# The up-projection of a gated MLP as seven half-size block products, with its weights split once and kept in DRAM

## The chip, the cores and the metric

The kernel runs on one core of one Trainium2 chip. The metric is the device time of one execution in microseconds (us); a profile of one execution shows what each engine did: TensorE (PE, its weight loads PEld), VectorE (DVE), ScalarE (ACT), GpSimd (POOL) and the DMA queue of SyncE (SP).

## The reference, cut to what matters

One layer: token mixing (projections, sparse attention, a pooling mixer, an output projection), a LayerNorm, then the part that the change rewrites:

```
def conv_ffn(x, conv_w, conv_b, w_up, w_down):
    h = x @ w_up                                     # (2048,1024) @ (1024,5632)
    h = causal depthwise conv, width 3, over time (h) + conv_b
    gate, val = jnp.split(h, 2, axis=-1)
    return (jax.nn.silu(gate) * val) @ w_down        # (2048,2816) @ (2816,1024)
x = layer_norm(ALPHA * x + ffn, ln2_g, ln2_b)
```

All is float32. The kernel takes each float32 operand as two fp32r parts, high and low, and makes every product of three matmuls (high by high, high by low, low by high): `mm3`, line 311.

## The kernel before, in words

The stages follow one another: projections, attention (`attention`, line 1193), the output projection with the first LayerNorm (`mix_out`, line 1249), the MLP (`ffn`, line 1398). Each stage is a Python generator that emits instructions for all engines in one order, and every engine runs its own in that order. `big` is a pool of 42 SBUF buffers of 4 KB a partition from which nearly all tiles come (`T`, line 260); a DMA load on SP can start when its buffer has been left by the last reader. PSUM is eight banks: four single ones (`PS1`, line 276) and two pairs (`PS2`, line 279). A result that goes to DRAM is put on a list by `store` and issued on SP two calls of `turn` later (lines 317 and 332).

**Attention.** For each block of 128 queries and each half of the heads (a unit) `values` (line 1094) walks over the key blocks, one step each, 272 steps in all: PE transposes the weights, ACT and DVE split them, PE multiplies by the values; the scores of the next unit are made between. POOL splits queries and outputs, and widens the reciprocal sums that PE transposes in `tail` (line 1119). The selection of the last key blocks, on DVE and ACT, is still under way when attention starts.

**The end of the output projection.** For the last 512 rows `mix_out` goes row block by row block; between them `ffn_ahead` (line 1321) loads rows of the normed x, transposes them on PE and splits them.

**The MLP.** The 2048 tokens are done in two halves of 1024. For each of the NF = 22 blocks f of 128 hidden channels, PE projects gate and value (`project`, 2 parts x 2 groups of 512 tokens x 8 slices of 128 input channels x 3 = 96 matmuls), ACT and DVE make the convolution out of PSUM (`conv`), ACT the SiLU, POOL the product with the value and its low part (`hidden`). Then `down` multiplies the block before by its rows of w_down (8 row blocks x 2 column groups x 3 = 48 matmuls), and DVE adds each 128x512 result from PSUM to a sum in SBUF. The up and down weights are loaded from the inputs for each half and split, mostly by POOL. At the change of halves the next rows are transposed beside the last `down`, and the norms of the first half (`norm_stages`, line 1358) run beside the first blocks of the second.

## Time and profile before

| | |
|---|---|
| median of 3 runs | 3420.83 us (3418.41 to 3428.26) |
| profiled execution, its span | 3423.1 us |
| its engines, busy | PE 3310.3, PEld 2802.5, DVE 2211.0, ACT 1345.0, POOL 1107.0 us |
| DMA | 399.51 MB, 117 GB/s over the span |

The profiled execution is known by its span, 3423.1 us from the first to the last instruction; it lies among the three timed runs, 2.3 us over their median. Busy time of PE is modelled for pipelined matmuls, so idle time before an instruction, with what ended it, says more than a busy share.

### The profile page before, as it was taken

How to read it: one execution, taken by the hardware profiler on the slowest of the kernel's cores; microseconds unless marked ns; L12 is line 12 of the kernel's file. 1: busy time of each engine (PE TensorE's matmuls, PEld its weight loads, DVE VectorE, ACT ScalarE, POOL GpSimd, SP SyncE). 2: the span in 40 equal slices, each digit the busy share in tenths (PEclk: the TensorE clock that was granted, in tenths of full speed). 3: DMA queues.
4: the chain of work that ended last, by engine and by line, in shares of the span. 5: the costliest groups of instructions: out<-in, count | busy, mean ns of one | idle time of the engine just before them, and what ended most of it. 6: DMA issues, size and time to landing. Idle time of an engine off the chain costs nothing.

```text
span 3423.1 us, 45344 instructions
## 1 busy us (share of the span) xinstructions
PE 3310.3 (97%) x16710; PEld 2802.5 (82%) x16710; DVE 2211.0 (65%) x4477; ACT 1345.0 (39%) x2520; POOL 1107.0 (32%) x1050
## 2 busy tenths in 40 slices
PE   8997899999999899999999999999999999999997
PEld 8886788888898788888788788888888778888886
DVE  5589878987888877777766544344444745445356
ACT  3466747746776666666410211111111411111113
POOL 3147410010012431111311334453443444354452
PEclk9998899999999999999999999999999999999999
DMA  8457755752765111000533521111112321111111
GB/s 317 139 204 269 254 199 198 267 194 88 277 220 166 62 42 31 30 28 7 201 126 142 188 78 40 53 43 50 56 44 86 129 87 44 50 50 43 56 44 68
DMA packets 237052, 399.51 MB, mean 117 GB/s; under 512 B 14938, under 2 KB 151070, under 8 KB 236830
## 3 DMA queue, kind: packets, MB, share of 16 engines
q1 hardware_dynamic: 227038, 378.79, 32.5%
q10 hardware_dynamic: 9792, 17.83, 1.4%
q8 instruction: 131, 2.15, 0.3%
q14 instruction: 91, 0.75, 0.1%
HBM read 289.44 MB, written 107.12 MB: 116 GB/s over the span
## 4 chain that ended last, share of the span: by engine, by line
PE 69%; DVE 6%; issue 2%; ACT 1%; POOL 1%; DMA 0%; POOLq 0%; SPq 0%; DVEq 0%; ACTq 0%
PE p L134 69%; DVE b L134 4%; DVE m L134 1%; ACT b L134 1%; POOL b L134 0%; DMA q<-m 0%; DMA b<-in_w_ffn_down_dram 0%; POOL nr L134 0%; DVE nt L134 0%; ACT m L134 0%; DVE t L134 0%; DVE nd L134 0%; DVE rinv L134 0%; DVE ab L134 0%; DVE bn L134 0%
## 5 line engine op out<-in xcount | busy, mean ns | idle before, releaser
L134 PE MATMUL p<-b,b 128*128 128x512 f32 (+2 forms) x14448 | 3077.8, 371 | 48.1 <-ACT b L134 21.6
L134 PEld LDWEIGHTS p<-b,b 128*128 128x128 f32 x14448 | 2512.8, 190 | 497.8 <-ACT b L134 24.5
L134 POOL TENSOR_TENSOR b<-b,b 128x1024 fp32r<-128x1024 f32 (+4 forms) x429 | 732.2, 1715 | 730.1 <-DVE b L134 610.9
L134 DVE TENSOR_TENSOR b<-b,p 128x512 f32<-128x512 f32 x608 | 380.9, 685 | 283.5 <-PE p L134 283.4
L134 ACT ACTIVATE b<-p 128x512 fp32r<-128x512 f32 (+9 forms) x658 | 395.3, 622 | 374.1 <-PE p L134 345.2
L134 DVE SCALAR_TENSOR_TENSOR b<-p,cw,b 128x1022 f32<-128x1022 f32 (+4 forms) x188 | 227.9, 1212 | 433.1 <-ACT b L134 432.1
L134 POOL TENSOR_SCALAR b<-b 128x1024 fp32r<-128x1024 f32 (+3 forms) x346 | 260.4, 761 | 646.3 <-ACT b L134 323.1
L134 ACT ACTIVATE b<-p,cw 128x1024 f32<-128x1024 f32 (+1 forms) x94 | 108.3, 1152 | 842.8 <-PE p L134 730.1
L134 ACT ACTIVATE m<-b,F 128x448 bf16<-128x448 f32 (+3 forms) x448 | 365.9, 819 | 81.8 <-DVE F L134 72.0
L134 DVE TENSOR_SCALAR_CACHE_REDUCE m<-b,F 128x512 bf16<-128x512 f32 (+6 forms) x476 | 371.1, 809 | 16.1 <-DMA q<-m 11.3
L134 ACT ACTIVATE b<-b 128x1024 fp32r<-128x1024 f32 (+3 forms) x130 | 130.8, 1011 | 342.2 <-POOL b L134 156.5
L134 DVE TENSOR_TENSOR b<-p,b 128x512 fp32r<-128x512 f32 (+1 forms) x306 | 222.4, 733 | 65.5 <-ACT b L134 62.7
L134 PE MATMUL p<-ident,b 128*128 128x128 f32 x1456 | 216.5, 277 | 21.1 <-ACT b L134 13.6
L134 PEld LDWEIGHTS p<-ident,b 128*128 128x128 f32 x1456 | 176.3, 142 | 55.2 <-ACT b L134 16.1
L134 DVE CUSTOM_DVE_ANT_0 b<-p,b 128x1024 f32<-128x1024 f32 (+7 forms) x192 | 174.3, 909 | 67.8 <-PE p L134 64.7
L134 ACT ACTIVATE b<-b,mx 128x1024 f32<-128x1024 f32 (+7 forms) x192 | 171.4, 895 | 42.6 <-DVE mx L134 37.3
L134 DVE SCALAR_TENSOR_TENSOR b<-b,ws,b 128x768 f32<-128x768 f32 (+5 forms) x154 | 157.2, 1049 | 41.8 <-ACT b L134 39.5
L134 PE MATMUL p<-kst,b 128*128 128x384 f32 (+3 forms) x656 | 150.5, 360 | 4.7 <-DVE b L134 3.6
L134 PEld LDWEIGHTS p<-kst,b 128*128 128x128 f32 x656 | 110.7, 189 | 21.2 <-ACT b L134 7.5
L134 POOL COPY b<-halo 128x16 f32<-128x16 f32 x16 | 2.8, 197 | 307.6 <-PE p L134 307.5
L134 ACT ACTIVATE m<-p 128x512 f32<-128x512 f32 x120 | 69.8, 593 | 76.5 <-PE p L134 61.6
L134 DVE TENSOR_TENSOR b<-b,b 128x1024 fp32r<-128x1024 f32 (+9 forms) x65 | 71.6, 1108 | 30.7 <-ACT b L134 22.6
(109 smaller groups left out, 1210.3 us busy)
## 6 DMA issues: line engine op xcount, KB each, us to landing
b<-wp SPq DMA_DIRECT2D x192, 512.0 KB, 6.0
b<-in_w_ffn_up_dram SPq DMA_DIRECT2D x88, 512.0 KB, 4.5
wp<-b SPq DMA_DIRECT2D x64, 512.0 KB, 5.5
b<-in_w_ffn_down_dram SPq DMA_DIRECT2D x44, 512.0 KB, 3.8
b<-in_w_in_dram SPq DMA_DIRECT2D x32, 512.0 KB, 6.5
xT<-b SPq DMA_DIRECT2D x32, 512.0 KB, 5.7
b<-xT SPq DMA_DIRECT2D x32, 512.0 KB, 6.1
b<-gm SPq DMA_DIRECT2D x32, 512.0 KB, 6.8
```

The lines of the kernel that those rows point to most:

```text
L134: return f(*args, **kw)
```

## The change

**Seven products.** The up-projection of two blocks of 128 hidden channels for 1024 tokens is a 2x2 block product: two halves of the 1024 input channels, two channel blocks, two groups of 512 tokens. Instead of eight block products, Strassen's seven are made: each is 4 slices of 128 input channels x 3 = 12 matmuls on sums or differences of blocks. A unit u is such a pair of channel blocks; a half of the tokens has 22 units (gates and values in turn), 154 products. Four PSUM banks hold the seven: products 5, 4 and 7 accumulate in the banks of 3, 2 and 1 (`BANK`, `OPENS`). `evacuate` puts the outputs together in SBUF on DVE and ACT; the convolution then reads SBUF.

**Sums of x.** For each j of four, `x_turn` transposes two slices of 128 channels for 1024 tokens (16 transposes), and `x_mix` makes the seven operands, sums first, then high and low parts. For the first half this lies in `mix_last`, which replaces the last part of `mix_out`; for the second in the last quarter of `down_half(0)`. The LayerNorm of the last four row blocks moves into the first unit.

**Sums of weights.** `up_weights` makes 154 tiles (22 units x 7, 512 KB each with high and low part) and stores them to DRAM: the first 98 during attention, all on POOL, from three buffers that take the place of constants no longer needed (`early_pool`, `late_pool`); the other 56 during the first up half, 0.6 a product, high parts on ACT. Each product's tile is fetched five products ahead (`up_fetch`), in both halves.

**The hidden channels** go to DRAM (`d_h`, 44 stores of 512 KB). **Down-projection:** `down_half` runs after each up half; for each of 2 x 2 groups of 512 tokens and 512 columns it accumulates over all 22 blocks in PSUM, in four banks, so that the sums in SBUF fall away. Each chunk of h and of w_down (256 KB each) is loaded and split (ACT the high part, DVE and POOL half of the low part each), two chunks ahead. In the very last group the last six blocks are done row block by row block.

The diff, cut to its core; the removed `ffn` is printed with the kernel above:

```diff
+TAIL = ("D--", "A--", "D--", "A--")
+ORDER = (3, 2, 1, 6, 5, 4, 7)
+BANK = {3: 0, 5: 0, 2: 1, 4: 1, 1: 2, 7: 2, 6: 3}
+OPENS = (3, 2, 1, 6)
+X_PLAIN = {2: 0, 5: 3}
+X_SUMS = {3: (1, 3, OP.subtract), 1: (0, 3, OP.add), 6: (1, 0, OP.add), 4: (2, 0, OP.subtract), 7: (2, 3, OP.add)}
+W_PLAIN = {3: 0, 4: 3}
+W_SUMS = {2: (2, 3, OP.add), 1: (0, 3, OP.add), 6: (2, 0, OP.subtract), 5: (0, 1, OP.add), 7: (1, 3, OP.subtract)}
+UP_AHEAD = 5
+W_BEFORE, W_FROM, W_RATE = 14, 4, 0.6
+LASTK = 6
...
     def attention(self):
+        self.early_pool.release()
+        self.late_pool = self.tc.alloc_tile_pool(name="latep", bufs=3)
+        self.w_inside, self.wcredit = W_BEFORE, 0.0
+        self.wgen = self.up_weights()
+        rate = W_BEFORE * len(ORDER) / (self.ends[-1] - W_FROM)
...
+                if tpos > W_FROM:
+                    self.up_more(rate)
...
+    def mix_last(self, mixed, ys, gb):
...
+        self.x_load(0, 0)
+        plan = {(0, 2): [lambda: self.x_turn(0)],
+                (0, 3): self.x_mix(0, 0, 2), (0, 4): self.x_mix(0, 2, 4),
+                (0, 5): self.x_mix(0, 4, 6), (0, 6): self.x_mix(0, 6, 7),
+                (1, 0): [lambda: self.x_load(0, 1)],
+                (1, 2): [lambda: self.x_turn(1)] + self.x_mix(1, 0, 1),
+                (1, 3): self.x_mix(1, 1, 4) + [lambda: self.x_load(0, 2)],
+                (1, 4): self.x_mix(1, 4, 7),
+                (1, 5): [lambda: self.x_turn(2)] + self.x_mix(2, 0, 2) + [lambda: self.x_load(0, 3)],
+                (1, 6): self.x_mix(2, 2, 7) + [lambda: self.up_fetch(0)],
+                (1, 7): [lambda: self.x_turn(3)] + [lambda i=i: self.up_fetch(i) for i in range(1, UP_AHEAD)]}
...
+        for c in range(2):
+            cs = slice(c * 512, (c + 1) * 512)
+            acc = [self.PS1() for _ in range(RB)]
+            for dc in range(DC):
...
+                for f in plan.get((c, dc), ()):
+                    f()
...
+            for rb in range(RB):
+                nc.vector.scalar_tensor_tensor(ys[rb][:, cs], ys[rb][:, cs], ALPHA, acc[rb], op0=OP.mult, op1=OP.add)
+        for f in self.x_mix(3, 0, 7):
+            f()
...
+    def combine(self, t, a, b=None, op=None, add=None, low=None, high=None):
+
+        nc = self.nc
+        if op is not None:
+            s = self.M(list(t.shape[:1]) + list(t.shape[2:]))
+            add.tensor_tensor(s, a, b, op=op)
+            a = s
+        if high is None:
+            nc.scalar.activation(t[:, 0], a, AF.Copy)
+        else:
+            high.tensor_scalar(t[:, 0], a, 1.0, 1.0, op0=OP.mult, op1=OP.mult)
...
+        for r in raw:
+            ps = self.PS2([P, 2, G])
+            for i in range(2):
+                for rb in range(RB):
+                    nc.tensor.transpose(ps[:, i, rb * P:(rb + 1) * P], r[:, i * RB + rb], self.ident)
+            b += [ps[:, 0], ps[:, 1]]
+        for i in (0, 3):
+            s = self.M([P, G])
+            nc.scalar.activation(s, b[i], AF.Copy)
+            b[i] = s
+        self.xsrc[j] = b
...
+            else:
+                t = self.T([P, 2, G], F32R)
+            b = self.xsrc[j]
+            low = nc.gpsimd if m in (2, 5) else nc.vector
+            if m in X_PLAIN:
+                self.combine(t, b[X_PLAIN[m]], low=low)
+            else:
+                i, k, op = X_SUMS[m]
+                self.combine(t, b[i], b[k], op, nc.gpsimd if m == 1 else nc.vector, low)
+            self.xc[m, j] = t
+
+        return [lambda m=m: one(m) for m in ORDER[lo:hi]]
...
+    def up_weights(self):
...
+        nxt = load(0)
+        for n in range(NF):
+            r = nxt
+            a = (r[0][:, :, :P], r[1][:, :, :P], r[0][:, :, P:], r[1][:, :, P:])
+            for s, m in enumerate(ORDER):
+                if s == 4 and n + 1 < NF:
+                    nxt = load(n + 1)
+                inside = n >= self.w_inside
+                t = (self.T if inside else self.L)([P, 2, 4, P], F32R)
+                high = None if inside else nc.gpsimd
+                if m in W_PLAIN:
+                    self.combine(t, a[W_PLAIN[m]], low=nc.gpsimd, high=high)
+                else:
+                    u, v, op = W_SUMS[m]
+                    self.combine(t, a[u], a[v], op, nc.gpsimd, nc.gpsimd, high)
+                self.store(self.d_w[n * len(ORDER) + s], t.bitcast(F32))
+                yield
+
...
+    def up_fetch(self, i):
+        t = self.uw[i] = self.T([P, 2, 4, P], F32R)
+        self.nc.sync.dma_start(t.bitcast(F32), self.d_w[i % len(self.d_w)])
...
+        def product(i, ps, m, js):
...
+            for j in js:
+                x = self.xc[m, j]
+                self.mm3(ps, w[:, 0, j], w[:, 1, j], x[:, 0], x[:, 1], j == 0 and m in OPENS, j == 3, m not in OPENS)
...
+        def evacuate(m, ps, st):
+            if m == 3:
+                st["s3"] = self.M([P, G])
+                nc.scalar.activation(st["s3"], ps, AF.Copy)
+            elif m == 2:
+                st["d"] = self.M([P, G])
+                nc.vector.tensor_tensor(st["d"], st["s3"], ps, op=OP.subtract)
+            elif m == 1:
+                st["e"] = self.M([P, G])
+                nc.vector.tensor_tensor(st["e"], st["d"], ps, op=OP.add)
+            elif m == 6:
+                st["h2"] = self.T([P, 2 * G])
+                nc.vector.tensor_tensor(st["h2"][:, G:], st["e"], ps, op=OP.add)
+            elif m == 5:
+                st["h1"] = self.T([P, 2 * G])
+                nc.scalar.activation(st["h1"][:, G:], ps, AF.Copy)
+                nc.vector.tensor_tensor(st["d"], st["d"], ps, op=OP.subtract)
+            elif m == 4:
+                nc.scalar.activation(st["h2"][:, :G], ps, AF.Copy)
+                nc.vector.tensor_tensor(st["d"], st["d"], ps, op=OP.add)
+            else:
+                nc.vector.tensor_tensor(st["h1"][:, :G], st["d"], ps, op=OP.add)
+
...
+            def first(i):
+                h, ch = st[f"h{i}"], part * NF + 2 * p + i - 1
+                v = a[i] = self.T([P, 2 * G])
+                nc.scalar.activation(v, h, AF.Identity, bias=cw[:, 3, ch:ch + 1], scale=cw[:, 2, ch:ch + 1])
+                nc.vector.scalar_tensor_tensor(v[:, 1:], h[:, :2 * G - 1], cw[:, 1, ch:ch + 1], v[:, 1:],
+                                               op0=OP.mult, op1=OP.add)
...
+            for s, m in enumerate(ORDER):
+                i = n * len(ORDER) + s
+                if i + UP_AHEAD < (hf + 1) * NF * len(ORDER):
+                    self.up_fetch(i + UP_AHEAD)
+                self.up_more(W_RATE)
+                if s in pending:
+                    pending[s]()
+                if u == 0 and s >= 3 and self.unnormed:
+                    self.unnormed.pop(0)()
+                if u == 0 and s < 4:
+                    product(i, banks[BANK[m]], m, range(3))
+                    if s == 3:
+                        for k in range(4):
+                            product(i - 3 + k, banks[BANK[ORDER[k]]], ORDER[k], [3])
+                            evacuate(ORDER[k], banks[BANK[ORDER[k]]], st)
+                else:
+                    product(i, banks[BANK[m]], m, range(4))
+                    evacuate(m, banks[BANK[m]], st)
+                if u == NF - 1 and s >= 4:
+                    self.down_ahead(hf, s - 4)
+                yield 2.7
+            pending = conv(st, n % 2, u // 2)
+        self.pending = pending
...
+    def down_load(self, hf, i):
+        q, c, k = i // (2 * NF), i // NF % 2, i % NF
+        t = self.draw[i] = self.T([P, 2, G])
+        self.nc.sync.dma_start(t[:, 0], self.d_h[hf][k][:, q * G:(q + 1) * G])
+        self.nc.sync.dma_start(t[:, 1], self.a["w_ffn_down"][0, k * P:(k + 1) * P, c * G:(c + 1) * G])
+
+    def down_split(self, i):
+        nc = self.nc
+        t = self.draw.pop(i)
+        hi, lo = self.T([P, 2, G], F32R), self.T([P, 2, G], F32R)
+        nc.scalar.activation(hi, t, AF.Copy)
+        nc.vector.tensor_tensor(lo[:, 0], t[:, 0], hi[:, 0].bitcast(F32), op=OP.subtract)
+        nc.gpsimd.tensor_tensor(lo[:, 1], t[:, 1], hi[:, 1].bitcast(F32), op=OP.subtract)
+        self.dparts[i] = (hi, lo)
...
+                    part = self.dparts.pop(i)
+                    if final and k >= NF - LASTK:
+                        held.append((k, part))
+                    else:
+                        for rb in range(RB):
+                            down(acc, k, rb, part)
+                    if hf == 0 and q == 1 and c == 1:
+                        for f in self.ahead_up.get(k, ()):
+                            f()
+                    norm_tick()
+                    if not held:
+                        yield 2.7
+                for rb in range(RB):
...
+                    nc.vector.scalar_tensor_tensor(ys[rb][:, cs], ys[rb][:, cs], ALPHA, acc[rb], op0=OP.mult, op1=OP.add)
+                    if c == 1:
+                        norm((hf * 2 + q) * RB + rb, ys[rb], TAIL[rb] if final else "A--")
+                    if held:
+                        yield 2.7
+        if hf == 0:
+            for f in self.x_mix(3, 0, 7):
+                f()
+        while norming:
+            norm_tick()
+            yield 1.0
...
+    def ffn(self):
+        yield from self.up_half(0)
+        n = NF * len(ORDER)
+        self.ahead_up = {1: [lambda: self.x_load(1, 0)], 3: [lambda: self.x_turn(0)], 4: self.x_mix(0, 0, 3),
+                         5: self.x_mix(0, 3, 5) + [lambda: self.x_load(1, 1)], 6: self.x_mix(0, 5, 7),
+                         8: [lambda: self.x_turn(1)], 9: self.x_mix(1, 0, 3),
+                         10: self.x_mix(1, 3, 5) + [lambda: self.x_load(1, 2)], 11: self.x_mix(1, 5, 7),
+                         13: [lambda: self.x_turn(2)], 14: self.x_mix(2, 0, 3),
+                         15: self.x_mix(2, 3, 5) + [lambda: self.x_load(1, 3)],
+                         16: self.x_mix(2, 5, 7) + [lambda: self.up_fetch(n)],
+                         19: [lambda: self.x_turn(3)],
+                         21: [lambda i=i: self.up_fetch(n + i) for i in range(1, UP_AHEAD)]}
+        yield from self.down_half(0)
+        yield from self.up_half(1)
+        yield from self.down_half(1)
...
-    def ffn(self):
```

## Rows read from the trace of the kernel before

**Rows 1.** The page: busy time, share of the span and instructions of each engine; then the chain of work that ended last, by engine.

```profile
PE 3310.3 (97%) x16710; PEld 2802.5 (82%) x16710; DVE 2211.0 (65%) x4477; ACT 1345.0 (39%) x2520; POOL 1107.0 (32%) x1050
...
PE 69%; DVE 6%; issue 2%; ACT 1%; POOL 1%; DMA 0%; POOLq 0%; SPq 0%; DVEq 0%; ACTq 0%
```

**Rows 2.** Busy time in stretches: attention, the start of the MLP, its first half, the change of halves, the second half, and what follows the last matmul. Columns: us, then busy us (instructions) of PE, PEld, DVE, ACT, POOL, the granted clock, DMA share, GB/s.

```profile
1143.00:1660.00 517.00, 507.32 (x2912) 431.83 (x2911) 382.41 (x774) 332.97 (x636) 118.56 (x112) 0.99 0.12 36
...
1944.00:2000.00 56.00, 52.42 (x235) 42.03 (x234) 25.65 (x32) 14.66 (x24) 18.96 (x15) 0.97 0.39 135
2000.00:2650.00 650.00, 650.00 (x2871) 537.97 (x2870) 295.24 (x401) 97.05 (x124) 302.57 (x162) 1.00 0.18 53
2650.00:2730.00 80.00, 77.15 (x360) 63.28 (x359) 67.41 (x100) 35.14 (x50) 30.20 (x20) 0.98 0.33 110
2730.00:3358.00 628.00, 624.06 (x2748) 513.85 (x2746) 284.47 (x443) 87.22 (x78) 293.07 (x156) 1.00 0.19 57
...
3406.20:3423.10 16.90, 0.00 (x0) 0.00 (x0) 12.17 (x28) 5.65 (x10) 4.58 (x3) 0.60 0.34 135
```

**Rows 3.** Timeline of ACT in the first half of the MLP: the first step of the convolution, which starts when a part's projection is done. Columns: start, us, engine, line, operation, output and input.

```profile
2157.92 1.21 ACT L134 ACTIVATE b<-p,cw 128x1024 f32<-128x1024 f32 x1 [5.93 <-issue]
2179.66 1.21 ACT L134 ACTIVATE b<-p,cw 128x1024 f32<-128x1024 f32 x1 [13.79 <-PE p L134]
...
2190.59 1.21 ACT L134 ACTIVATE b<-p,cw 128x1024 f32<-128x1024 f32 x1 [5.93 <-issue]
```

**Rows 4.** All waits of PE from 1900 us to the end: total us, times, longest.

```profile
PE p L134 <- DVE b L134: 5.1, 4, 2.7
PE p L134 <- POOL b L134: 2.8, 3, 1.3
PE p L134 <- ACT b L134: 2.4, 2, 1.2
```

**Rows 5.** Groups of DVE instructions, forms apart: busy us, mean ns of one, idle before.

```profile
L134 DVE TENSOR_TENSOR b<-b,p 128x512 f32<-128x512 f32 x608 | 380.9, 685 | 283.5 <-PE p L134 283.4
L134 DVE TENSOR_TENSOR b<-p,b 128x512 fp32r<-128x512 f32 x280 | 190.8, 688 | 54.5 <-ACT b L134 51.9
L134 DVE SCALAR_TENSOR_TENSOR b<-p,cw,b 128x1023 f32<-128x1023 f32 x82 | 105.2, 1283 | 403.8 <-ACT b L134 403.8
L134 DVE SCALAR_TENSOR_TENSOR b<-b,nr,b 128x1024 f32<-128x1024 f32 x14 | 22.1, 1588 | 0.1
```

**Rows 6.** The same for ACT.

```profile
L134 ACT ACTIVATE b<-p,cw 128x1024 f32<-128x1024 f32 x82 | 99.0, 1207 | 787.4 <-PE p L134 674.7 <-issue 112.7
...
L134 ACT ACTIVATE b<-b 128x1024 f32<-128x1024 f32 x41 | 43.3, 1056 | 63.2 <-DVE b L134 58.4 <-DVE nt L134 4.8
L134 ACT ACTIVATE b<-p 128x512 f32<-128x512 f32 x64 | 37.6, 593 | 23.0 <-PE p L134 15.3 <-issue 6.5 <-ACT b L134 0.2
...
L134 ACT ACTIVATE m<-b,nm 128x1024 bf16<-128x1024 f32 x14 | 16.1, 1147 | 14.9 <-DVE nm L134 14.8
L134 ACT ACTIVATE m<-b 128x1024 bf16<-128x1024 f32 x14 | 14.7, 1048 | 8.4 <-DVE b L134 8.2
```

**Rows 7.** The same for POOL.

```profile
L134 POOL TENSOR_TENSOR b<-b,b 128x512 fp32r<-128x512 f32 x30 | 38.8, 1293 | 2.4
L134 POOL TENSOR_SCALAR b<-b 128x512 fp32r<-128x512 f32 x30 | 23.0, 766 | 321.6 <-ACT b L134 321.6
...
L134 POOL TENSOR_TENSOR nr<-nv,mhalf 128x1 f32<-128x1 f32 x16 | 14.7, 919 | 82.8 <-DVE nm L134 59.8 <-DVE nv L134 23.0
L134 POOL COPY m<-rinv 128x256 f32<-128x256 f32 x32 | 12.6, 413 | 42.6 <-DVE rinv L134 42.6
```

**Rows 8.** Timeline in attention: POOL's widening of the sums for a `tail`, and PE's transposes of it.

```profile
1351.09 0.75 POOL L134 COPY m<-rinv 128x256 f32<-128x256 f32 x2
...
1352.88 0.60 PE L134 MATMUL p<-ident,m 128*128 128x128 f32 x4
```

**Rows 9.** Timeline at the start of attention: DVE instructions with two inputs in SBUF beside POOL's, and PE after them (in brackets, its idle time and what ended it).

```profile
1159.98 2.34 POOL L134 TENSOR_TENSOR b<-b,b 128x1024 fp32r<-128x1024 f32 x1
1160.15 2.19 DVE L134 TENSOR_TENSOR t<-F,st 128x2 f32<-128x2 f32 x1
...
1163.14 1.94 PE L134 MATMUL p<-b,b 128*128 128x512 f32 x6 [3.08 <-DVE mx L134]
...
1181.38 1.27 POOL L134 TENSOR_TENSOR b<-b,b 128x512 fp32r<-128x512 f32 x1
1181.38 1.28 DVE L134 SCALAR_TENSOR_TENSOR nd<-b,fx,cg 128x1 f32<-128x1 f16 x1
...
1183.32 2.02 PE L134 MATMUL p<-b,b 128*128 128x512 f32 x5 [1.14 <-DVE nd L134]
```

**Rows 10.** One tile in attention, the sum of two partial sums (both in SBUF) on DVE: duration in ns, least, median and most.

```profile
L134 DVE TENSOR_TENSOR rinv<-ssum x16: 156/158/1486, 1284.2 to 1643.2; 128x4 f32<-128x4 f32 x16
```

**Rows 11.** Three stretches of 10 us in which the DMA engines are busy throughout; columns as in Rows 2. In the first, rows of 1 KB are loaded and rows of 4 KB stored, in the second mostly rows of 4 KB are stored, in the third loaded.

```profile
210.00:220.00 10.00, 9.43 (x40) 6.90 (x39) 8.84 (x32) 7.71 (x25) 9.76 (x21) 1.00 1.02 324
320.00:330.00 10.00, 10.00 (x45) 8.26 (x44) 9.82 (x6) 1.92 (x6) 10.00 (x19) 1.00 1.03 415
...
1680.00:1690.00 10.00, 10.00 (x46) 8.29 (x45) 9.28 (x10) 4.29 (x6) 5.93 (x4) 1.00 1.03 413
```

**Rows 12.** DMA issues of the page: output and input, count, size, median us from issue to landing.

```profile
b<-wp SPq DMA_DIRECT2D x192, 512.0 KB, 6.0
b<-in_w_ffn_up_dram SPq DMA_DIRECT2D x88, 512.0 KB, 4.5
```

**Rows 13.** Waits of SP's own DMA queue from 2000 to 3350 us: line, what it waited for, us in total, times, longest.

```profile
SPq L193 <- PE p L134: 1151.6, 77, 22.5
```

More of the change, by code (lines that the diff above doesn't have):

```diff
@@ L271, in C, with E @@
         return self.const.tile(shape, dt, tag=n, name=n)
+    def E(self, shape, dt=F32, name="e"):
+        n = self._name(name)
+        return self.early_pool.tile(shape, dt, tag=n, name=n)
     def sml(self, shape, dt=F32, tag="t", bufs=None):
@@ L309, in split_new, with mm3 @@
         return hi, lo
-    def mm3(self, ps, ah, al, bh, bl, first, last):
+    def mm3(self, ps, ah, al, bh, bl, first, last, more=False):
+        kw = {"skip_group_check": True} if more else {}
         mm = self.nc.tensor.matmul
-        mm(ps, ah, bh, start=first, stop=False)
-        mm(ps, ah, bl, start=False, stop=False)
-        mm(ps, al, bh, start=False, stop=last)
+        mm(ps, ah, bh, start=first, stop=False, **kw)
+        mm(ps, ah, bl, start=False, stop=False, **kw)
+        mm(ps, al, bh, start=False, stop=last, **kw)
     def store(self, dst, src):
@@ L370, in tables @@
         nc.vector.tensor_copy(posf, self.posi)
[L371 removed]
+        inv = self.E([P, ROT], name="inv")
         for i, f in enumerate(FREQS):
@@ L427, in setup @@
         self.d_at = [self.DT([P, 4, G], name="at") for _ in range(NG)]
-        self.d_x1 = [self.DT([P, D], name="x1") for _ in range(NB)]
+        self.d_x1 = [self.DT([NB // 2, P, D], name="x1") for _ in range(2)]
+        self.d_h = [[self.DT([P, 2 * G], name="h") for _ in range(NF)] for _ in range(2)]
         self.I = {}
@@ L1298, in mix_out @@
                 ys.append(y)
-            if g + 1 < NG:
-                nxt = load_at(g + 1)
-            else:
-                pre = Share(self.ffn_ahead(), 7, 5)
+            if g + 1 == NG:
+                yield from self.mix_last(mixed, ys, gb)
+                return
+            nxt = load_at(g + 1)
             for rb in range(RB):
@@ L1347, in ffn_ahead @@
         nc.vector.tensor_copy(self.cw, ps[:, :, :2 * NF])
-        self.xrows = self.x1_rows(0, 1, range(EARLY))
-    def x1_rows(self, hf, q, rbs=range(RB)):
+    def combine(self, t, a, b=None, op=None, add=None, low=None, high=None):
[8 more added lines that the diff above has]
+            high.tensor_scalar(t[:, 0], a, 1.0, 1.0, op0=OP.mult, op1=OP.mult)
+        low.tensor_tensor(t[:, 1], a, t[:, 0].bitcast(F32), op=OP.subtract)
@@ L1351, in x1_rows, with L, x_load @@
+    def L(self, shape, dt):
+        return self.late_pool.tile(shape, dt, tag="l4", name=self._name("l"))
+    def x_load(self, hf, j):
         t = []
-        for rb in rbs:
-            r = self.T([P, D])
-            self.nc.sync.dma_start(r, self.d_x1[hf * 8 + q * RB + rb])
+        for k in (j, j + 4):
+            r = self.T([P, NB // 2, P])
+            self.nc.sync.dma_start(r, self.d_x1[hf][:, :, k * P:(k + 1) * P].rearrange("b p c -> p b c"))
             t.append(r)
-        return t
+        self.xraw[j] = t
@@ new lines, in x_turn @@
+    def x_turn(self, j):
+        nc = self.nc
+        raw = self.xraw.pop(j)
+        b = []
+        for r in raw:
[9 more added lines that the diff above has]
+        self.xsrc[j] = b
@@ new lines, in x_mix, with one @@
+    def x_mix(self, j, lo, hi):
+        def one(m):
+            nc = self.nc
+            if m == 7 and j < 3:
+                t = self.L([P, 2, G], F32R)
+            else:
[9 more added lines that the diff above has]
+        return [lambda m=m: one(m) for m in ORDER[lo:hi]]
@@ new lines, in up_weights, with load @@
+    def up_weights(self):
+        nc = self.nc
+        up = self.a["w_ffn_up"][0].rearrange("(k p) c -> p k c", p=P)
+        self.d_w = [self.DT([P, 2, 4, P], name="uw") for _ in range(NF * len(ORDER))]
+        def load(n):
+            c0 = n % 2 * DFF + n // 2 * 2 * P
+            t = [self.T([P, 4, 2 * P]) for _ in range(2)]
+            for k in range(2):
+                nc.sync.dma_start(t[k], up[:, 4 * k:4 * k + 4, c0:c0 + 2 * P])
+            return t
+        nxt = load(0)
[15 more added lines that the diff above has]
+                yield
@@ new lines, in up_more, with down_ahead @@
+    def up_more(self, rate):
+        self.wcredit += rate
+        while self.wcredit >= 1:
+            self.wcredit -= 1
+            next(self.wgen, None)
+    def down_ahead(self, hf, step):
+        if step == 0:
+            self.draw, self.dparts = {}, {}
+        self.down_load(hf, step)
+        if step:
+            self.down_split(step - 1)
+    def down_load(self, hf, i):
[3 more added lines that the diff above has]
+        self.nc.sync.dma_start(t[:, 1], self.a["w_ffn_down"][0, k * P:(k + 1) * P, c * G:(c + 1) * G])
@@ L1613, in run @@
         self.settle()
+        self.late_pool.release()
 @with_exitstack
```

314 lines of the change are left out of this document (110 added, 204 removed).

## The prediction

> **What bounds the kernel now.** I read the page first: PE is busy for 3310 of 3423 us, and the chain that ended last runs through PE for 69% [rows 1]. A share of the whole can hide stages with other limits, so the stretches come next. In attention PE idles 9.7 of 517 us; in the MLP it never waits from 2000 to 2650 us, 2.9 us around the change of halves, 3.9 us in the second half and 3.6 us at the start; then come 16.9 us without matmuls [rows 2]. DVE is busy for less than half of the MLP, DMA for a fifth. So the MLP is PE's alone, and a change is worth what it takes from PE less what it makes PE wait for.
>
> The price of a matmul is not the mean of its row, since pipelined matmuls overlap. The convolution starts at 2157.92 and again at 2190.59 us, one block f later [rows 3]: 32.67 us for 96 + 48 = 144 matmuls of 512 columns, 0.2269 us each. The step for one part alone (48 matmuls, 2179.66 to 2190.59) gives 0.2277, so the up and the down matmuls cost the same.
>
> **The change part by part.**
>
> *Seven for eight.* Before, the up-projection takes 2 x 22 x 96 = 4224 matmuls; after, 2 x 22 x 7 x 12 = 3696. The 2112 of the down-projection stay, the transposes too (64 a half). 528 x 0.2269 = 119.8 us less on PE. The operands keep type and size, so I take the same price.
>
> *Putting the seven together.* A unit lasts 84 x 0.2269 = 19.1 us. DVE has six additions with one operand in PSUM (0.685), four convolution steps from SBUF (taken at the 1.283 of the PSUM form) and one product a unit (taken alike): 4.1 + 5.1 + 1.3 = 10.5 us [rows 5]. ACT has three copies (0.593), two convolution starts (1.207) and one SiLU (1.056): 5.3 us [rows 6]. Units alternate between bank sets, and a bank is used twice inside a unit only three or four products (8 us) apart. Cost on PE: none, with 8.6 us of DVE to spare in each unit; without that cover a late evacuation would stop PE at products 5, 4 or 7.
>
> *Weight sums in attention.* A tile takes POOL 0.766 for the high part, 1.293 for the low part and in five of seven cases 1.293 for the sum: 2.98 us, and 98 tiles 292 us [rows 7]. With the 118.6 us that POOL has there already it is busy for 411 of 517 us [rows 2], so it keeps up. What is queued behind it waits: the copies for `tail` end 1.0 us before PE transposes them [rows 8]. There are 32 copies [rows 7], two a `tail`, so 16 tails. If POOL is inside a weight tile with chance 0.56 and a uniform rest of it delays the copies, PE waits 0.37 us in the mean, 6 us together; bounds 0 and 16 x 2 = 32.
>
> The second price is DVE's. At 1160 us a DVE addition of 128x2, with two inputs in SBUF, lasts 2.19 us beside a POOL instruction of 2.34, and PE then idles 3.08; at 1181 one of 128x1 lasts 1.28 beside one of 1.27, and PE idles 1.14 [rows 9]. POOL will be busier in just that stretch, the end of the selection: I add 5 us (bounds 0 and 15, five such pairs). Later such additions come once a unit, at most 1.49 us for 0.158 [rows 10]; DVE has a quarter of its time free there [rows 2]: 2 us (0 to 8). The Trainium skill (SBUF — State Buffer, Who interferes with whom) gives a rule that speaks against this change: a DVE instruction with two SBUF inputs and a GpSimd instruction that reads SBUF exclude one another for the whole instruction. By that rule the convolution, which moves from PSUM to SBUF, and the low parts become exposed to POOL too, and the additions with an operand in PSUM don't. Attention: +13 us (0 to 55).
>
> *Start of the MLP.* In `mix_last`, the operands of one j take DVE nine instructions of 0.69, ACT nine of 0.6 and POOL three of 1.29. The third j has 5.4 us of PE's work as cover and needs about 8, so `x_turn(3)` waits some 3 us for its banks; then the additions of the last four banks and the fourth j stand on DVE, partly covered by the 36 matmuls (8.2 us) that need only three j. I take 7 us of idle time in place of 3.6: +3.4 (bounds 0 and +10).
>
> *Supply of weights.* Bytes for a product in the first 93: a fetch of 0.524 MB, 0.6 of a store, 0.09 of raw weights, 0.075 of hidden channels: 1.004 MB in 2.723 us, 369 GB/s. Busy DMA engines move 413 to 415 GB/s in rows of 4 KB, 324 with rows of 1 KB among them [rows 11]; nine tenths here are of 4 KB, so I take it as just enough. A fetch issued five products ahead has 13.6 us, against 6.0 to land [rows 12]; but loads on SP wait for buffers that PE leaves [rows 13], and the 42 are nearly all in use, so the lead is shorter. The stores wait on POOL on the same queue, with the fetches behind them. Bounds: 0, and at 324 GB/s 3.098 - 2.723 = 0.375 us for each of 93 products, 35 us. I take +3, near the rows of 4 KB. The Trainium skill (HBM Reference, Specifications (TRN2)) gives an effective 358 GB/s per core; this trace shows more, 415, and decides. By 358 this term would be an estimated 7 us. After the 93 the demand is 0.599 MB a product, 220 GB/s.
>
> *Down-projection.* A chunk's 12 matmuls last 2.72 us; its split takes ACT 1.06, DVE 0.69, POOL 1.29. Even if DVE and POOL exclude one another, 1.98 of 2.72. In the last quarter of `down_half(0)` the operands of three j come on top, 5 x 0.69 + 3 x 1.29 = 7.3 us of such work each: 22 x 1.98 + 22 = 65.6 in 59.9 us. Two chunks split ahead cover 5.4 us: +4 (0 to 15). The sums on SBUF (608 additions) fall away [rows 5], and four bank evacuations a group hide behind 36 matmuls.
>
> *Change of halves and stalls of before.* PE's waits from 1900 us sum to 10.3 [rows 4], of which 3.6 are counted above; 6.7 go. At the new change of halves four norms (10 us of ACT) stand ahead of the first evacuations: 5 us come (2 to 10). Net -1.7.
>
> *End.* After the last matmul come one evacuation (0.69), a norm's two ACT passes (1.05, 1.15), POOL's power (0.92), one DVE pass (1.59 with its waits) [rows 5 to 7], small steps and the store: about 12 us for 16.9, -4.9 (-8 to +3).
>
> **Sum.** -119.8 + 13 + 3.4 + 3 + 4 - 1.7 - 4.9 = -103.0 us. The profiled execution's 3423.1 becomes 3320.1; it lies 2.3 us over the median of the runs, so I forecast 3318 us.
>
> **The rivals.**
>
> *Starved of weights.* The stretch of 93 products runs at the 324 GB/s of mixed rows: 35 us in place of 3, 3350 us. For it: stores, small rows and fetches on one queue. Against it: two of the three busy stretches are at 413 GB/s or more [rows 11].
>
> *POOL coupled to attention.* Tails and DVE pay nearer to their upper bounds, 45 in place of 13: 3350 us. For it: PE was stopped by exactly this pair of engines [rows 9]; against it: most of DVE's time in attention goes to instructions with an operand in PSUM.
>
> *The products don't run dense.* Each of 308 products waits, for an evacuation or its tile, 0.3 us: 92 us, 3410 us; the change would not do what it says. Against it: the cover of 8.6 us a unit.
>
> *Slower: POOL sets the pace of attention.* If each weight instruction takes twice its row, held off by DVE's instructions with two SBUF inputs and by its three buffers, a tile costs 5.96 us, POOL needs 118.6 + 584 = 703 us in a stage of 517, and since the stages are in order, the end moves by 186 instead of 13: 3491 us. It decides from 5.3 us a tile, where attention grows by the 116 us that the rest gains. Against it: POOL's row of 1.293 contains such waits already, and DVE's instructions in attention mostly have an operand in PSUM.
>
> **How the numbers follow.** The forecast has 0.75, starvation 0.09, the coupling 0.09, products with gaps 0.03, slower 0.04. The range goes from 3296, where attention, supply and start cost nothing, to 3362, past the two rivals at 3350 and a little of each together. About 0.3%, 10 us, is what a measurement can tell from no change: faster holds the first three cases and half of the fourth, 0.945, the same 0.015, slower 0.04.
>
> **What would show it.** The matmuls' count falls by 528 and the price stays 0.227 us; two units take 38.1 us. Attention's stretch grows by about 13 us, with PE's idle time put down to POOL or DVE at the tails and before 1215 us. In the first 13 units DMA shares stay under 1 and PE doesn't wait for DMA; waits for DMA there say starvation. Waits of PE for DVE or POOL in the last quarter of the first down half say the shared pair. If attention grows by more than 55 us, or a unit lasts over 20 us after the 93rd product, the prediction is wrong.

## The result, and the profile after

The changed kernel takes 3348.33 us (median of four runs, 3344.69 to 3350.98) for 3420.41 us before, a ratio of 0.9784 with an interval of 0.9769 to 0.9799. That is faster and inside the range, but 30 us above the forecast of 3318. The profiled execution spans 3342.9 us for 3423.1: 80 us gained of the 103 summed.

The first view is the page: PE's matmuls fall by 528, from 16710 to 16182, as forecast, and PE's busy time by 97, not by 120.

```profile
PE 3213.2 (96%) x16182; PEld 2703.1 (81%) x16182; DVE 2326.4 (70%) x4378; ACT 1606.5 (48%) x2876; POOL 1208.8 (36%) x1269
...
PE 55%; DVE 5%; issue 2%; POOL 1%; ACT 1%; DMA 1%; SPq 0%; POOLq 0%; DVEq 0%; ACTq 0%
```

Next, busy time in stretches, columns as in [rows 2]: the first half's units while weights are still made (two rows; the first unit begins at 1945.2 us), the same units afterwards, the change of halves, the second half's units.

```profile
1950.00:2000.00 50.00, 41.20 (x161) 32.62 (x160) 34.09 (x38) 17.89 (x30) 33.52 (x40) 0.90 0.74 265
2000.00:2250.00 250.00, 237.36 (x1004) 190.86 (x1004) 143.24 (x132) 89.58 (x144) 125.69 (x82) 0.97 0.92 333
2250.00:2400.00 150.00, 150.00 (x655) 121.63 (x654) 81.13 (x89) 45.31 (x64) 0.50 (x1) 1.00 0.63 232
2600.00:2700.00 100.00, 94.07 (x417) 74.96 (x416) 80.94 (x100) 49.15 (x74) 48.15 (x31) 0.97 0.57 201
2700.00:3090.00 390.00, 390.00 (x1700) 316.52 (x1700) 214.51 (x304) 111.25 (x125) 3.47 (x3) 1.00 0.59 218
```

The reader is to see where POOL is busy: from 1950 to 2250 us PE idles 8.8 + 12.6 us and the granted clock falls to 0.90 and 0.97; from 2250 to 2400, with POOL done, PE is never idle, and from 2400 to 2600, where the down-projection begins, for 1.7 us. All waits of PE from 1900 us (for [rows 4]):

```profile
PE p L140 <- DVE b L140: 12.5, 11, 4.8
PE p L140 <- DVE m L140: 8.9, 4, 5.0
PE p L140 <- DMA b<-uw: 5.5, 2, 3.8
PE p L140 <- ACT b L140: 3.1, 1, 3.1
PE p L140 <- POOL b L140: 1.8, 3, 0.8
```

31.8 us where it was 10.3, and two thirds are put down to DVE, not to fetches (`b<-uw`). From 1950 to 2250 us alone PE is idle for 21.4 us.

Four marks of the timeline split the span: DVE's first pass over attention scores (1108.3 before, 1102.8 after), its first gate product in `mix_out` (1675.6 and 1674.3), the first down matmul (2403.0, after only), PE's end (3406.1 and 3331.5).

| stage, us | before | after | change | forecast |
|---|---|---|---|---|
| up to attention | 1108.3 | 1102.8 | -5.5 | 0 |
| attention | 567.3 | 571.5 | +4.2 | +13 |
| `mix_out` and MLP | 1730.5 | 1657.2 | -73.3 | -111.1 |
| after the last matmul | 17.0 | 11.4 | -5.6 | -4.9 |

The first stage isn't touched by the change; in the kernels below it ends anywhere from 1102.0 to 1111.6 us, so these 5.5 us are scatter. This profile is the fastest of the four runs. The 37.8 us that the third row is short are what has to be explained.

### The profile page after: what moved, and what is told of

The parts are those of the page before. It is cut to its first block, busy times and chain, and to the rows that moved or that the text cites. A ratio compares the mean times of both kernels' runs of the same rounds, so it can differ in the third digit from the quotient of the medians.

```text
span 3342.9 us, 47116 instructions
## 1 busy us (share of the span) xinstructions
PE 3213.2 (96%) x16182; PEld 2703.1 (81%) x16182; DVE 2326.4 (70%) x4378; ACT 1606.5 (48%) x2876; POOL 1208.8 (36%) x1269
## 4 chain that ended last, share of the span: by engine, by line
PE 55%; DVE 5%; issue 2%; POOL 1%; ACT 1%; DMA 1%; SPq 0%; POOLq 0%; DVEq 0%; ACTq 0%
PE p L140 55%; DVE b L140 4%; ACT b L140 1%; DVE m L140 1%; POOL b L140 1%; DMA b<-in_w_ffn_down_dram 0%; DMA h<-b 0%; DMA b<-uw 0%; ACT m L140 0%; POOL lt L140 0%; POOL nr L140 0%; POOL l L140 0%; POOL lr L140 0%; POOL lv L140 0%; DVE nt L140 0%
## 5 line engine op out<-in xcount | busy, mean ns | idle before, releaser
L140 PE MATMUL p<-b,b 128*128 128x512 f32 (+2 forms) x12820 | 2843.3, 369 | 65.5 <-ACT b L140 21.8
L140 PEld LDWEIGHTS p<-b,b 128*128 128x128 f32 x12820 | 2206.4, 191 | 471.6 <-ACT b L140 23.9
L140 POOL TENSOR_TENSOR b<-b,b 128x512 fp32r<-128x512 f32 (+3 forms) x408 | 529.4, 1318 | 690.2 <-DMA b<-x 408.1
L140 ACT ACTIVATE b<-b 128x1024 fp32r<-128x1024 f32 (+2 forms) x270 | 275.8, 1029 | 354.3 <-DMA b<-in_w_ffn_down_dram 138.0
L140 DVE TENSOR_TENSOR b<-b,b 128x512 fp32r<-128x512 f32 (+4 forms) x268 | 320.0, 1220 | 102.4 <-ACT b L140 78.9
L140 DVE TENSOR_TENSOR m<-m,p 128x512 f32<-128x512 f32 x176 | 120.6, 685 | 271.4 <-ACT b L140 207.0
L140 PE MATMUL p<-b 128*128 128x512 f32 x704 | 271.3, 390 | 0.4 <-DVE b L140 0.4
L140 DVE SCALAR_TENSOR_TENSOR b<-b,cw,b 128x1023 f32<-128x1023 f32 (+1 forms) x176 | 248.4, 1413 | 30.6 <-ACT b L140 28.9
L140 POOL TENSOR_SCALAR b<-b 128x256 fp32r<-128x256 f32 (+3 forms) x216 | 117.7, 559 | 370.6 <-DMA b<-in_w_in_dram 168.1
L140 PEld LDWEIGHTS p<-b 128*128 128x128 f32 x704 | 132.1, 188 | 28.5 <-DVE b L140 1.2
```

The costliest lines, as they stand in the source:

```text
L140: return f(*args, **kw)
```

## The experiments

For each kernel two durations from its own timeline stand beside the median: attention (as above) and the first half, from the first gate product to the first down matmul (728.7 us in after).

| kernel | median us | ratio (interval) | attention | first half |
|---|---|---|---|---|
| after | 3348.3 | 0.9784 (0.9769 to 0.9799) | 571.5 | 728.7 |
| no_sums | 3314.4 | 0.9678 (0.9661 to 0.9696) | 569.2 | 699.7 |
| attn_only | 3319.1 | 0.9692 (0.9676 to 0.9708) | 577.1 | 696.0 |
| inside_no_dma | 3324.1 | 0.9712 (0.9690 to 0.9735) | 570.6 | 707.9 |
| inside_no_pool | 3332.4 | 0.9729 (0.9712 to 0.9747) | 578.6 | 706.9 |
| high_pool | 3343.3 | 0.9764 (0.9742 to 0.9785) | 579.5 | 726.0 |
| late_only | 3347.8 | 0.9795 (0.9781 to 0.9809) | 572.0 | 728.4 |
| single_banks | 3328.4 | 0.9715 (0.9694 to 0.9736) | 579.4 | 704.6 |
| banks_high | 3321.7 | 0.9702 (0.9683 to 0.9720) | 574.7 | 701.0 |
| banks_late | 3313.0 | 0.9672 (0.9652 to 0.9693) | 578.6 | 695.6 |
| banks_late_12 | 3307.4 | 0.9658 (0.9644 to 0.9673) | 569.2 | 693.4 |
| banks_18 | 3358.4 | 0.9808 (0.9790 to 0.9827) | 618.1 | 698.4 |

**What the weight sums cost, and where.** Four kernels leave parts of them out, and their fetches read tiles made earlier.

```diff
 no_sums:        -for n in range(NF):  +for n in range(1):      fetch d_w[i % 7]
 attn_only:      -for n in range(NF):  +for n in range(W_BEFORE):  fetch d_w[i % 98]
 inside_no_dma:  +if not inside: store(...)   raw loads only for n < W_BEFORE, fetch d_w[i % 98]
 inside_no_pool: +if inside: store(d_w[...], r[s % 2]); yield; continue      fetch d_w[i % 98]
```

no_sums: 

> Leaves out the sums, raw loads and stores of 147 of the 154 weight tiles; all fetches read the same seven. After the change the trace has 12.6 us of idle PE from 2000 to 2250 us and three stretches at half clock there. Theory A (the sums made during the first 13 units cost some 20 us, those in attention nothing): 3328 us, the first wait of PE in mix_out still within 2 us of 1667, from 2000 to 2250 no idle time and a clock of 1.00. Rival B (attention too pays for its 98 tiles, the 13 us of the forecast, hidden so far by something else): 3315 us, with mix_out starting some 13 us sooner. Rival C (the loss after 2000 us is the products' own evacuations): within 5 us of 3348.

attn_only: 

> After the change, with the 98 weight tiles made during attention and none of the 56 later ones (their raw loads, sums and stores are left out; the fetches read earlier tiles). Beside no_sums (3314 us) it prices the sums in attention alone. Between the first exp and the first mix product the traces so far took 571 to 579 us with the 98 sums (seven kernels, the middle one 579) and 567 and 569 without. If the middle is right: 3324 us, and the 56 later tiles cost the other 24 of 34. If the one trace of after is right (2 to 4 us): 3317, and the later ones cost 31. If the forecast's 13 is right: 3327.

inside_no_dma: 

> Keeps the arithmetic of the 56 tiles made during the first half's units, leaves out their raw loads and stores (the fetches read earlier tiles). If POOL and ACT hold up DVE and so the banks (theory A1), most of the loss stays: 3340 us or more, with PE waits for DVE from 2000 to 2250 us. If SP's queue or the memory holds up the fetches (A2), 3328 to 3333 us and no such waits.

inside_no_pool: 

> Keeps the raw loads and as many stores of the same size for those 56 tiles (raw data is stored), leaves out their sums, high and low parts on POOL and ACT. A1 (POOL and ACT hold up DVE): 3328 to 3333 us, no waits of PE for DVE from 2000 to 2250 us. A2 in its form of memory bandwidth: 3340 us or more, with waits for fetched tiles; in its form of SP waiting on POOL: also 3328 to 3333, since the stores no longer wait.

no_sums gains 34 us, not 20. That is theory B's figure (3315) but not its place: `mix_out` starts at 1674.3 us in both, and the first half is 29 us shorter, so the sums made during units cost more than I had read off the idle time. attn_only puts attention's share at 4.6 us by the medians (the intervals overlap) and 8 by its timeline, between 2 and 13. One trace says little here: in the nine kernels that make the same 98 tiles in attention the stage takes 570.6 to 579.5 us, 577.1 in the middle. Neither A1 nor A2 alone survives: without transfers the first half is 21 us shorter, without arithmetic 22, without both 29 to 33. Either load by itself thus costs 7 to 12 us, both together about 30. Something links them. A1's sign failed too: in inside_no_pool POOL is at rest from 2000 to 2250 us, and PE still waits 7.6 us for DVE there; in inside_no_dma, with POOL at work for 125 us, 0.4.

**One-bank tiles.** The timeline of PE in the second half shows one place where units differ (columns: start, us, operation, output and inputs, count); `l` holds the hidden state's part of product 7:

```profile
2718.25 2.24 PE L140 MATMUL p<-l,b 128*128 128x512 f32 x9
2720.32 14.76 PE L140 MATMUL p<-b,b 128*128 128x512 f32 x63
2734.92 1.79 PE L140 MATMUL p<-l,b 128*128 128x512 f32 x7
2736.55 2.96 PE L140 MATMUL p<-b,b 128*128 128x512 f32 x12
2739.35 0.63 PE L140 MATMUL p<-l,b 128*128 128x512 f32 x2
...
2756.82 2.24 PE L140 MATMUL p<-l,b 128*128 128x512 f32 x9
```

In one unit its nine matmuls stand together; in the next, whose banks are halves of two two-bank tiles, twelve of another product stand between seven and two. The order of PE's instructions in the built program says more; the framework that builds it doesn't keep to the order in which the kernel emits them, though I wrote so of the kernel before. By their first matmuls the products of such a unit stand as 3, 1, 2, 5, 6, 7, 4 where the kernel writes 3, 2, 1, 6, 5, 4, 7, and some are split. Product 2, in the second half of the tile that product 3 uses, stands four matmuls behind 3 and waits for ACT (3's evacuation), where in the other units it waits for its weights alone. Between 6 and 7, which share the other tile, stand only some matmuls of 5 and at times of the next unit's 3.

```diff
-            t = [self.PS2([P, 2, G]) for _ in range(2)]
-            banks = [t[0][:, 0], t[0][:, 1], t[1][:, 0], t[1][:, 1]]
+            banks = [self.PB() for _ in range(4)]      # one-bank tiles, p2 released after attention; x_turn likewise
```

> From mix_out on, four one-bank tiles stand in place of the two tiles of two banks, so that a product into one bank doesn't wait for the evacuation of the other bank of its tile. In the trace of after, the eight products from 2756.6 to 2778.8 us take 22.2 us in place of 21.8, while the others take 2.72 each. Theory D (the two-bank tiles make the price of every second unit): two units take 38.1 us in place of 38.6, 22 pairs give 10 us, 3338 us, and less if the stalls before 2250 us shrink too. Rival (the seven products' hand-overs cost this whatever the tiles): two units stay at 38.6 us and the time at 3348.

3328.4 us: 20 gained where I expected 10, and not by the units' price (two units take 38.26 us now, from 2705.79 to 2744.05, for 38.57, from 2718.25 to 2756.82 above; I expected 38.1). It comes from the first half, 24 us shorter, and PE's waits from 1950 to 2250 us change their kind. After (first fence) and single_banks (second):

```profile
PE p L140 <- DVE m L140: 8.1, 3, 5.0
PE p L140 <- DVE b L140: 7.9, 3, 4.8
PE p L140 <- DMA b<-uw: 5.5, 2, 3.8
```

```profile
PE p L140 <- DMA b<-uw: 10.7, 13, 2.8
```

No wait for an evacuation is left; 13 waits for fetched tiles are. The new transposes of `x_turn` are not the reason: from `mix_out`'s first gate product to the first unit all the kernels take 267 to 271 us.

In after all six waits for DVE (16.0 us) fall in units with two-bank tiles: one at product 5, two at 4, three at 7, each for the evacuation of the other bank of its tile. The first, PE and then DVE:

```profile
1961.68 2.24 PE L140 MATMUL p<-l,b 128*128 128x512 f32 x9
1963.76 9.14 PE L140 MATMUL p<-b,b 128*128 128x512 f32 x39
1977.86 8.41 PE L140 MATMUL p<-b,b 128*128 128x512 f32 x24 [4.97 <-DVE m L140]
```

```profile
1974.95 2.26 DVE L140 SCALAR_TENSOR_TENSOR b<-b,lr,b 128x1024 f32<-128x1024 f32 x1 [0.90 <-POOL lr L140]
1977.13 1.47 DVE L140 TENSOR_TENSOR m<-m,p 128x512 f32<-128x512 f32 x2
```

Behind the first unit's product 7 (`l`) come its last three matmuls and 36 of the second unit's 3, 1 and 2; then 5 waits for 2's evacuation, the first of the two at 1977.13. That stands on DVE behind a pass of the LayerNorm that the change moved here.

**The queue of the fetches.** In after SP waits for POOL for half of the stretch from 2000 to 2250 us, at the stores of weight tiles (first row), with fetches (L1461) behind:

```profile
SPq L353 <- POOL b L140: 126.4, 42, 6.9
SPq L1461 <- PE p L140: 18.0, 11, 4.0
```

Stores that are issued later, and sums that finish sooner (POOL makes the high part, so it needn't wait for ACT), each with two-bank and with one-bank tiles:

```diff
 late_only, banks_late:  -self.store(d_w, t)   +if inside: self.after(4, lambda: sync.dma_start(d_w, t))
 high_pool, banks_high:  -high = None if inside else nc.gpsimd   +high = nc.gpsimd
```

high_pool: 

> After the change as it is, but POOL makes the high part of the late 56 tiles too, so that no sum waits for ACT. Theory A1b (the hand-over POOL to ACT to POOL, with ACT held by a SiLU that waits for DVE, makes the stores late and blocks SP): SP's 126 us of waits for POOL from 2000 to 2250 us fall below 60, and the time comes to 3335 us. Rival (two-bank tiles make PE wait for DVE, whatever POOL does; more POOL work only slows DVE further): 3345 us or more, PE's waits for DVE stay at 10 us or more in that stretch.

banks_late: 

> One-bank tiles, and the stores of the late 56 tiles are issued four products later, by when POOL is done. single_banks was 3328 us with 10.7 us of PE waits for fetched tiles, SP waiting 121 us for POOL from 2000 to 2250 us and DMA at 350 GB/s. Queue theory (fetches stand behind stores that wait for POOL): SP's waits for POOL go to under 30 us, PE's waits for fetched tiles to under 3, 3319 us. Memory theory (350 GB/s is what it moves): PE's waits for fetched tiles stay at 8 us or more, 3328 us.

banks_high: 

> One-bank tiles, and POOL makes the high parts of the late 56 tiles. Queue theory: sums are done sooner, the fetches get past: 3321 us, PE's waits for fetched tiles under 5 us. Memory theory: 3328, 10 us of such waits. If POOL slows DVE more than it saves: 3332, with PE waits for DVE.

late_only: 

> The late stores of banks_late with the two-bank tiles of after: the fourth corner of a square (after 3348, single_banks 3328, banks_late 3313 us). If the two causes add up: -15 as on top of one-bank tiles, 3333 us, with PE still waiting for DVE from 2000 to 2250 us. If the two-bank tiles turn each late fetch into a longer stall (the loss of both together is more than the sum): 3328 or less. If without one-bank tiles the queue was not what ended last: 3343 or more.

With two-bank tiles neither does much: late_only cuts SP's waits for POOL to a sixth (sum of its rows 21.0 us; SP now waits 95.0 for buffers that PE leaves) and its time stays; high_pool brings them to 53.8 and 3343.3 us, its interval overlapping that of after, and PE still waits 18.8 us for DVE from 1950 to 2250. With one-bank tiles the same edits give 15 us (the intervals just clear each other) and 7 (within them). So the 126 us that I had read as a cause were none of the loss in after, though they were the next in line. SP and PE in late_only, 2000 to 2250 and 1950 to 2250 us:

```profile
SPq L1457 <- POOL b L140: 13.3, 10, 3.5
```

```profile
PE p L140 <- DVE b L140: 8.5, 5, 2.3
PE p L140 <- DVE m L140: 7.3, 4, 5.8
PE p L140 <- DMA b<-uw: 7.1, 4, 3.3
```

And the stretches of banks_late, the columns as above:

```profile
1950.00:2000.00 50.00, 45.64 (x214) 37.46 (x213) 38.69 (x49) 20.05 (x34) 35.57 (x41) 0.99 0.68 234
2000.00:2250.00 250.00, 250.00 (x1094) 205.99 (x1093) 155.95 (x148) 97.25 (x159) 125.53 (x87) 0.99 0.97 365
```

The same work of POOL, PE not idle for 250 us, and DMA at 365 GB/s where after moved 333 and single_banks 350: what memory moves was not the limit, and the queue theory holds. Its signs came out less cleanly than its time: SP still waits 39.6 us for POOL in banks_late (sum of its rows; under 30 expected) and PE 4.4 us for fetches before 2000 us, though none after; in banks_high 94.2 and 7.4.

**More and fewer tiles in attention.**

```diff
-W_BEFORE, W_FROM, W_RATE = 14, 4, 0.6
+W_BEFORE, W_FROM, W_RATE = 18, 4, 0.6     # banks_18, on single_banks; 12 in banks_late_12, on banks_late
```

banks_18: 

> One-bank tiles, 126 in place of 98 weight tiles made during attention. Queue and memory theory alike: the crowded stretch of the MLP shrinks to about half, PE's waits for fetched tiles from 10.7 to 5 us: -5. What attention pays decides the rest: from its first exp to the first mix product it took 571 to 579 us with the sums and 567 to 569 without. If that is per tile: +2, in all 3325 us. If POOL, busy for some 493 of 517 us then, holds the tails up: +15, in all 3338 us.

banks_late_12: 

> One-bank tiles and late stores as in banks_late (3313 us), with 84 weight tiles made in attention and 70 in the MLP in place of 98 and 56. If the attention's share grows with its tiles (about 10 us for 98, 47 for 126) and the crowded stretch of the MLP costs nothing once stores don't block: 3308 us, with the stage from the first exp to the first mix product at 575 or less. If the longer crowded stretch costs PE some waits for fetched tiles: 3313 or more.

28 tiles more cost attention 39 us beside single_banks, past my dearer case; 14 fewer take it to what it is without sums, 569.2 (one trace). In banks_18 more than half of the price is paid at the end, PE from 1640 to 1730 us (before that, PE's waits for DVE's `mx` grow from 4.6 in single_banks to 15.8):

```profile
PE p L140 <- ACT b L140: 10.1, 2, 8.9
PE p L140 <- POOL m L140: 9.5, 1, 9.5
```

The timelines of SP and of POOL there show why. SP stands at seven stores of weight tiles for 20 us, waiting for POOL, with the raw loads and `w_attn_branch` behind them; POOL waits 6.5 us for the latter, and the last sums and the copies for the last `tail` come after that.

```profile
1645.51 20.42 SPq L356 DMA_DIRECT2D uw<-l  x7
...
1672.96 2.21 SPq L1249 DMA_DIRECT2D b<-in_w_attn_branch_dram  x4
```

```profile
1671.20 1.29 POOL L140 TENSOR_TENSOR l<-b,l 128x512 fp32r<-128x512 f32 x1
1678.97 1.05 POOL L140 TENSOR_SCALAR b<-b 128x1024 fp32r<-128x1024 f32 x1 [6.49 <-DMA b<-in_w_attn_branch_dram]
...
1704.49 0.75 POOL L140 COPY m<-rinv 128x256 f32<-128x256 f32 x2
```

banks_late_12 met its expectation and has the lowest time here, 3307.4 us, 3.4% under before; the 5.6 us to banks_late lie within the intervals.

## Why the prediction was right in sign and 30 us off

**The step that failed** is in "Putting the seven together": that a bank is used twice inside a unit only three or four products (8 us) apart, so that 8.6 us of DVE's slack in each unit makes the evacuations free. It holds for the four one-bank tiles. In every second unit two banks share a tile, and the program orders accesses by tile, so that 2 follows the evacuation of 3, 5 that of 2, 4 that of 5 and 7 that of 6. Kernels that differ in their two-bank tiles alone differ by 20 us (after 3348.3, single_banks 3328.4), with 16.0 us of PE waits for DVE and none. The diff shows the two tiles; I counted banks and not tiles. The products at which I said that a late evacuation would stop PE, 5, 4 and 7, are those at which it did, and DVE had its slack (busy for 143 of 250 us): the distance was wrong, not the work. The longest stall from 2000 us on shows one chain (DVE, ACT, PE in turn):

```profile
2065.76 3.75 DVE L140 SCALAR_TENSOR_TENSOR b<-b,cw,b 128x1023 f32<-128x1023 f32 x2
2071.83 3.48 DVE L140 SCALAR_TENSOR_TENSOR b<-b,cw,b 128x1023 f32<-128x1023 f32 x2 [2.32 <-ACT b L140]
2075.24 0.68 DVE L140 TENSOR_TENSOR b<-m,p 128x512 f32<-128x512 f32 x1
```

```profile
2069.61 1.06 ACT L140 ACTIVATE b<-b 128x1024 f32<-128x1024 f32 x1 [7.21 <-DVE b L140]
2070.57 1.22 ACT L140 ACTIVATE b<-b,cw 128x1024 f32<-128x1024 f32 x1
```

```profile
2075.97 2.50 PE L140 MATMUL p<-l,b 128*128 128x512 f32 x5 [4.79 <-DVE b L140]
```

Beside POOL two convolution steps take 3.75 us in place of 2.6; ACT's SiLU waits 7.21 us for them, and the next convolution, on ACT and then on DVE, waits for the SiLU; behind that stands the evacuation of product 6 (`b<-m,p`, 2075.24), and product 7, in the other half of its tile, waits 4.79. With a bank's tile to itself it waits for product 1's evacuation, with three products between.

POOL alone doesn't make these stalls. In inside_no_pool the same two steps take 2.60 us, and product 7 of the same unit (2071.41 us) still waits 1.85. In inside_no_dma POOL lengthens the steps (1521 to 1610 ns in the mean for 1281 without it), the tiles are two-bank ones, and PE waits 1.0 us from 2000 to 2250 (its one long wait, 9.7 us, is at the second unit's product 5, as in after). There the two-bank units keep the pattern of seven, twelve and two matmuls from the fence above; in after none of the first six does, since matmuls of the next unit's product 3 stand before or among those of 7 and 4. After 2250 us, with the pattern back, the shared tiles cost 38.57 - 38.26 = 0.31 us a pair of units. So the link between the two loads may be that the late loads and stores change the order in which the framework places PE's products, and that in this order a delay reaches PE. That is inferred and not shown: no run changed the order alone.

**The clock** was in no term. After the longer of these stalls the granted clock is at the lower of its two levels (1.2 and 2.4 GHz) for some microseconds, while PE works again. Windows around the stall above and at the change of halves:

```profile
2076.00:2079.00 3.00, 3.00 (x7) 2.13 (x8) 0.69 (x1) 1.70 (x5) 1.29 (x1) 0.50 0.69 221
2080.00:2085.00 5.00, 5.00 (x24) 4.09 (x23) 2.38 (x3) 2.25 (x3) 2.12 (x2) 1.00 0.74 250
2666.40:2673.00 6.60, 6.02 (x13) 3.88 (x14) 6.60 (x8) 4.94 (x10) 3.31 (x2) 0.50 1.00 357
```

By the means of the stretches I estimate 0.10 x 50 + 0.03 x 250 = 12.5 us from 1950 to 2250, beside 21.4 us of idle time: stalls of 1 to 5 us cost PE about half as much again. The waits alone, which I would have read first, understate the loss.

**Term by term.** *Seven for eight*: the count is exact, the price is not. 38.57 us for 168 matmuls are 0.2296 each, 0.0027 over the 0.2269 taken: 10 us on 3696; with one-bank tiles (0.2277) 3 us. *Supply of weights*, +3: of the 12.6 us of idle time from 2000 to 2250 us 11.0 are waits for the evacuations above; of supply proper after shows 5.5 us of waits from 1950 on and single_banks 10.7, and the queue, which the term names and prices at next to nothing, is worth 15 us once the tiles are apart. The demand that I worked out, 369 GB/s, was met then (365 in banks_late, 372 at a DMA share of 0.99 in banks_late_12). *Start of the MLP*: nothing, for the 7 us taken. The first unit runs without a wait; the 8.8 us of idle time from 1950 to 2000 look like this term and are not: 4.97 are the second unit's product 5 (above), 3.83 a fetch, and 5 of clock follow. *Down-projection and change of halves*, 9 us: 5.9 idle and 3 of clock from 2600 to 2700, right in size together (1.6 of idle time up to 2650 for the 4 of the down-projection). *End*, 12 us: 11.4. *Attention*, +13: 4 in this trace, about 9 by the middle of the nine kernels with 98 tiles (577.1 for 567.3 and 569.2 without): somewhat high, within its scatter, and steep from 98 to 126 tiles. *The sum*: idle time and clock from 1950 to 2250 us (34) and the dearer matmuls (10) are 44 us where the terms had 10, the start and the supply; that is 34 of the 37.8 us. With both faults mended, banks_late takes 3309.64 + 0.83 - 1690.2 = 1620.3 us from the first gate product to PE's end, for the 1619.4 that the forecast's terms give (1730.5 - 111.1). That it fits within 1 us is luck: terms that were too high (the start) and too low (the matmuls) cancel.

**The rivals.** *Starved of weights* named 3350 us, and the time is 3348. It isn't borne out: PE waited for fetches for 5.5 us, and freeing the queue alone left the time where it was. A rival whose number comes true has still to show its own waits. *POOL coupled to attention*, also 3350: attention paid some 4 to 9 us, not 45. *Products not dense* comes nearest in kind, with 21.4 us of idle time in place of 92, and only in the units beside which weights are still made. *POOL sets the pace* didn't happen at 98 tiles; banks_18, with 126, pays 51 us in attention over before (POOL busy for 426.5 of 517), for the greater part through the end of the stage and the loads behind its stores, not by each tile's price.

What stays open: whether in units with two-bank tiles the waits themselves or the changed order of the products costs more (both went together), and with it what exactly joins the transfers and POOL's work in after.

## What to carry to other kernels

When a change lets PE return to an accumulator soon, count reuse distances by the object on which the program waits (the tile), not by the bank; two banks in one tile make neighbours wait for one another's evacuation. Where taking away either of two loads brings back most of the loss of both, look for the link between them before mending either: late stores were worth nothing until the banks were separate, and 15 us after. Compare the order in which an engine runs its instructions with the order in which the kernel writes them. And price a stall at more than its idle time, since the clock may come back later than the work.

## What the runs showed of the hardware

DVE's convolution steps, with both inputs in SBUF, are the ones that POOL lengthens; its sums with an operand in PSUM are not. DVE's groups in after, from 2000 to 2250 us (POOL busy for half of it) and, below the dots, from 2250 to 2380 (POOL idle), mean ns after the comma:

```profile
L140 DVE SCALAR_TENSOR_TENSOR b<-b,cw,b 128x1022 f32<-128x1022 f32 x24 | 42.5, 1770 | 0.7
L140 DVE TENSOR_TENSOR m<-m,p 128x512 f32<-128x512 f32 x48 | 32.9, 685 | 85.2 <-ACT b L140 42.2 <-PE p L140 38.4 <-POOL m L140 4.1
...
L140 DVE TENSOR_TENSOR m<-m,p 128x512 f32<-128x512 f32 x28 | 19.2, 686 | 44.9 <-ACT b L140 37.0 <-PE p L140 8.0
L140 DVE SCALAR_TENSOR_TENSOR b<-b,cw,b 128x1022 f32<-128x1022 f32 x14 | 18.0, 1282 | 0.3
```

1770 for 1282 ns, and 685 for 686. In inside_no_pool, with POOL at rest in the first stretch too, the same step takes 1281 ns there. The rule of the Trainium skill (SBUF — State Buffer, Who interferes with whom) on instructions with two SBUF inputs beside GpSimd's agrees with these rows, and it was right that the convolution, moved from PSUM to SBUF, would become exposed; "Putting the seven together" still took its steps at 1.283 us. The price was only paid where an evacuation stood behind the convolution and a product behind the evacuation: in banks_late the convolution runs beside the same POOL work (1722 ns), and PE waits for none of it.
